# Six instead of four layer-norm finals behind up-projection products, and early splits at the start of down-projection

## The chip, the cores and the metric

The kernel runs on one core of one Trainium2 chip. The metric is the device time of one execution in microseconds (us), and a kernel's time is the median of its runs. Engines are called as in the profile: PE (TensorE), DVE (VectorE), ACT (ScalarE), POOL (GpSimd) and SP (SyncE, whose queue issues nearly all the transfers named here).

## The reference

One layer of a hybrid decoder, sequence 2048, model width 1024, feed-forward width 4096, all in float32. Cut to what matters here:

```python
proj = x @ w_in[l]
y_a, y_b, y_c, y_d = rwkv7(...), dilated_attention(...), ssd(...), hgrn2(...)
mix = jnp.concatenate([y_a, y_b, y_c, y_d], axis=-1) @ w_out[l]
x = _layer_norm(ALPHA * x + mix, ln1_w[l], ln1_b[l])
h = jnp.square(jax.nn.relu(x @ w_up[l]))
x = _layer_norm(ALPHA * x + h @ w_down[l], ln2_w[l], ln2_b[l])
```

The change touches the last four lines: the output projection `w_out`, the first layer norm, and the two feed-forward products.

## The kernel before, in words

**Numbers.** A float32 operand is split into a high part, which ACT copies to the type that PE multiplies (`split`, by `copy`), and a low part, raw minus high, which DVE makes, or POOL for every third one. A matrix product then is three PE instructions: high x high, high x low, low x high. A tile is 128 tokens; there are 16.

**Output projection and finals.** In the attention stage `out_part(t)` multiplies the six 128-row pieces of a tile that don't come from attention by their part of `w_out` and stores the sum `zF`. When the tile's attention is done, `out_final4(t)` merges the attention branches, loads `zF` into a buffer `z2`, adds the last two pieces' products (12 PE instructions `mm<-wh,yah` and the like), does the layer norm `lnorm` on DVE and ACT, stores the tile, transposes it by PE in two groups of four (`ident,z`), and stores the transposed tile in DRAM (`x1T`). It is cut into four pieces by `yield`. This is called a *final* below, numbered by its tile. `weave` hands such pieces out between the attention units, and what is left over runs behind the last unit. Finals 8 to 11 are in the last `weave`; finals 12 to 15 run in up-projection, each in four pieces, behind products 7t+6, 7t+8, 7t+13 and 7t+14 (t = 0 to 3).

**Up-projection** (`ffn_up`) takes the tokens in two halves (1024 each), and each half in 16 steps. A step makes a 2 x 2 block product out of seven products P1 to P7 instead of eight (sums and differences of blocks go into each). A product is 12 PE instructions of 512 columns into one PSUM bank. The four weight blocks `wr` of a step are loaded and made into seven split operands (`wh`, `wl`; `ws` are sums) by `ffn_w`; the bank results go through DVE, POOL and ACT (`q`, `u`, `c`) and are stored as seven combinations in DRAM (`H0P`, `H1P`). The first half's inputs come from tiles 0 to 7 (`ffn_x`), the second half's from tiles 8 to 15 (`ffn_x1`, in pieces during the first half's steps 7 to 14).

**Weight preparation.** Down-projection needs sums and differences of `w_down` blocks. `ffn_t` makes them for f = 0 to 15 in four `next` calls each and stores them in `TD`: 12 to 15 and 0 to 4 during `out_part`, on POOL alone; 5 in up-projection's steps 5 and 6, 6 to 11 in the second half, with DVE doing two of the four.

**Down-projection** (`ffn_down`) has 32 steps of seven products (PE instructions `bank<-x1h,hh` and the like). The seven weights are loaded and split up front (`x0h`, `x0l`, `x1h`, `x1l`), later exchanged by `change`. The inputs H are loaded into `xr` or `z2` and split four products ahead into buffers `hh` and `hl` of a pool `fd`, which lies over the pool of up-projection's weights. Loads, splits and products are written in one order, and a scheduler sets each engine's order from it. Each engine, and SP's queue, takes its instructions strictly in that order.

Of the kernel before, what the change touches and what calls it, by code (L numbers as in the profile page):

```python
# [84 lines left out]
class Body:  # L85
# [28 lines left out]
    def tt(self, eng, out, a, b, op):  # L114
        (self.nc.gpsimd if eng == "g" else self.nc.vector).tensor_tensor(out, a, b, op=op)  # L115

# [6 lines left out]
    def sub(self, eng, out, a, b):  # L123
        self.tt(eng, out, a, b, ALU.subtract)

# [7 lines left out]
    def copy(self, eng, out, in_):  # L133
        if eng == "a":
            self.nc.scalar.activation(out, in_, AF.Copy)  # L135
        elif eng == "g":
            self.nc.gpsimd.tensor_copy(out, in_)
        else:
            self.nc.vector.tensor_copy(out, in_)

# [17 lines left out]

    def load_split(self, src, n):

        h, out = n // 2, []
        for i in range(2):
            hi, lo = (self.t(self.wp, t, [P, self.wlen // 2], F32R, bufs=self.wbufs)[:, :h] for t in ("wh", "wl"))
            raw = self.t(self.rp, "raw", [P, self.wlen // 2], bufs=self.rbufs)[:, :h]
            self.nc.sync.dma_start(raw, src[:, h * i : h * i + h])
            self.split(raw, hi, lo)
            out.append((hi, lo))
        return h, out
# [7 lines left out]
    def split(self, raw, hi, lo):  # L176

        self.copy("a", hi, raw)
        self.rr += 1
        self.sub("g" if self.rr % 3 == 0 else "v", lo, raw, hi.bitcast(F32))  # L180

# [910 lines left out]
    def out_open(self, es, ef):  # L1092
# [5 lines left out]
        self.xT = [self.dp.tile([KT, P, 512], F32, name=f"x1T{i}") for i in range(seq // 512)]  # L1098
        load = lambda ks: [self.load_split(self.ap["w_out"][k], D) for k in ks]

# [5 lines left out]
        self.rbufs, self.wbufs, self.wlen = 4, 12, D  # L1106
        wo = load((0, 1, 4, 5, 6, 7))
        self.wp, self.wbufs = self.of, 4
        self.wo = wo + load((2, 3))
        self.nc.sync.dma_start(self.ln1, self.ap["lns"][0:2].partition_broadcast(P))  # L1110
# [284 lines left out]
    def ffn_down(self):  # L1395

        nc, tc, of = self.nc, self.tc, self.of
        nsteps = 32
        lns = self.t(of, "ln1", [P, 2, D], bufs=1)
        wtag = lambda n: "x1" if n in ("P1", "P6", "P4", "P3") else "x0"  # L1400
        chunk = lambda n, i: (i - self.OFF[n]) // 4 % 4
        with ExitStack() as es:
# [21 lines left out]
            def split_h(m):  # L1424
                if m < len(seq):
                    H[m] = [self.t(fd, x, [P, 512], F32R, bufs=6) for x in ("hh", "hl")]
                    self.split(raws.pop(m), *H[m])

# [21 lines left out]
            def prod(m):  # L1450
# [3 lines left out]
                for a, b, w, c in change:  # L1454
                    if a == m:
                        raws[w] = list(load_w(w, c))
                    if b == m:
                        split_w(w, raws.pop(w))
                ps = self.slot("py", [P, 512])
# [7 lines left out]

            places = ("xr", "xr", "wl", "wh", "wl", "wh", "wl")
            for q, (n, place) in enumerate(zip(("P1", "P6", "P2", "P7", "P5", "P4", "P3"), places)):
                rs = load_w(n, chunk(n, 0), place)  # L1470
                if place == "xr":
                    W[n] = [self.split_to(wtag(n), r) for r in rs]
                else:
                    split_w(n, list(rs))
                if q == 1:
                    for m in range(7):
                        load_h(m)
                if 0 < q < 5:
                    split_h(q - 1)
            for m in (7, 8, 9):  # L1480
                load_h(m)
            ys += [self.t(fd, f"y2_{n}", [P, 512]) for n in range(5, 14)]
            two = self.t(of, "x1t", [P, 2, 512], bufs=1)
            ys += [two[:, 0], two[:, 1]]
            for i in range(nsteps):
                hf, v, p = i // 16, i % 16 // 4, i % 4
                y = [[ys[4 * p + 2 * l + j] for j in range(2)] for l in range(2)]
# [28 lines left out]
                if i == 2:  # L1516
                    nc.sync.dma_start(lns, self.ap["lns"][2:4].partition_broadcast(P))
                if v == 3:
# [23 lines left out]
def body(ctx, tc, ap, seq=SEQ):  # L1542
# [74 lines left out]
    part = lambda t: (B.out_part(t), 7)  # L1617
    T = B.ffn_t((12, 13, 14, 15, *range(5)), False)

    def part_t(t):  # L1620
        for i, _ in enumerate(B.out_part(t)):
            if i in (0, 2, 4, 6) or i == 5 and t % 2:
                next(T)
# [8 lines left out]
    X = B.ffn_x()  # L1632
    B.weave([], units[40:], [final(8 + t) for t in range(4)])
    ea.close()
    with ExitStack() as e1:
        B.t(pool("pad", e1, side="right"), "pad", [P, 504])
        B.fw = pool("fw", e1, side="right", reuse_waits="tile")
        X1 = B.ffn_x1()
        T = B.ffn_t(range(5, 12), True)
        behind = {}  # L1640
        for t in range(4):
            it = B.out_final4(12 + t)
            for p in (6, 8, 13, 14):
                behind.setdefault(7 * t + p, []).append(it)
        B.ffn_up(0, X, lambda s: next(T) if s in (5, 6) else next(X1) if s in (7, 8, 9, 10, 11, 12, 13) else None,
                 lambda s: next(T) if s in (5, 6) else next(X1) if s in (8, 9, 11, 12, 14) else None, behind)
        B.ffn_up(1, next(X1), lambda s: next(T) if 1 < s < 14 else None, lambda s: next(T) if 1 < s < 14 else None)
# [82 lines left out]
```

## Time and profile before

| what | value |
| --- | --- |
| runs | 3148.49, 3129.91, 3138.72 us; median 3138.72 |
| profiled execution | 3125.35 us, span 3123.5 us |
| mean granted PE clock | 0.935 |
| PE busy | 2889.3 us, 93% of the span |
| DVE, POOL, ACT busy | 2154.9, 1607.3, 1357.1 us |
| attention stage ends, up-projection starts | about 1743 to 1760 us |
| down-projection starts | 2467 us |

The profiled execution is one run, 13.4 us faster than the median. In a timeline row stand the start, the duration, the engine, the line, the operation, output<-inputs, the shape and the count; in brackets the engine's idle time just before it and what ended that.

### The profile page before, as it was taken

To read this page: it belongs to the slowest core of one execution; us is meant where nothing else is said; L and a number is where in the kernel's file an instruction comes from. 1 tells how busy PE (TensorE), PEld (TensorE's weight loads), DVE (VectorE), ACT (ScalarE), POOL (GpSimd) and SP (SyncE) were. 2 spreads that over 40 slices of the span, in tenths; PEclk is the share of its full clock that TensorE was granted. 3 is DMA by queue.
4 is the path that set the end of the run, shared out by engine and by line. 5 is a ranking of instruction groups with operands and counts; after the bars stand their busy time and mean duration, and the time that the engine had idled before them with its cause. 6 is when DMAs were issued, how large, how long until landed. Compare 5 with 4: busy or idle time off the path is not lost. (4 is left out here: it accounts for less than half of the span.)

```text
span 3123.5 us, 46758 instructions
## 1 busy us (share of the span) xinstructions
PE 2889.3 (93%) x15524; PEld 2346.8 (75%) x15524; DVE 2154.9 (69%) x3794; ACT 1357.1 (43%) x2910; POOL 1607.3 (51%) x1466
## 2 busy tenths in 40 slices
PE   8899989889899999899999699999999899999996
PEld 6567777777677778777777477787788688878885
DVE  3457589778867765533445777678776677799777
ACT  3334334433443453334334444455455544554454
POOL 1333366455645645530223744646644577678666
PEclk9899888999899999699999799999999899999998
DMA  5434333333343354684455556658855866568653
GB/s 170 131 114 107 107 97 102 117 102 91 112 114 90 115 168 125 240 263 146 140 175 168 180 175 192 202 157 249 252 160 156 267 222 192 192 201 265 196 189 125
DMA packets 406083, 512.67 MB, mean 164 GB/s; under 512 B 34257, under 2 KB 234065, under 8 KB 405585
## 3 DMA queue, kind: packets, MB, share of 16 engines
q1 hardware_dynamic: 405840, 509.68, 52.8%
q8 instruction: 123, 2.02, 0.3%
q14 instruction: 120, 0.97, 0.1%
HBM read 353.64 MB, written 155.91 MB: 163 GB/s over the span
## 5 line engine op out<-in xcount | busy, mean ns | idle before, releaser
L112 PE MATMUL mm<-xh,wh 128*128 128x512 f32 x672 | 284.8, 426 | 30.7 <-ACT xh L135 16.9
L112 PE MATMUL mm<-xl,wh 128*128 128x512 f32 x672 | 284.6, 424 | 6.4 <-DVE xl L115 3.1
L112 PE MATMUL mm<-xh,wl 128*128 128x512 f32 x672 | 280.8, 418 | 2.7 <-DVE wl L115 2.6
L135 ACT ACTIVATE wh<-raw 128x512 fp32r<-128x512 f32 (+1 forms) x220 | 136.6, 629 | 177.3 <-PE mm L112 73.0
L112 PE MATMUL bank<-x1h,hh 128*128 128x512 f32 x512 | 200.8, 392 | 10.5 <-ACT hh L135 10.5
L115 POOL TENSOR_TENSOR y<-y,wh 128x512 f32<-128x512 f32 x112 | 173.8, 1562 | 58.0 <-ACT wh L135 31.1
L112 PE MATMUL bank<-x1h,hl 128*128 128x512 f32 x512 | 200.5, 392 | 2.1 <-DVE hl L115 2.1
L112 PE MATMUL bank<-x1l,hh 128*128 128x512 f32 x512 | 200.7, 392 | 0.8 <-DVE x1l L115 0.8
L112 PEld LDWEIGHTS mm<-xh,wh 128*128 128x128 f32 x672 | 134.4, 200 | 71.1 <-ACT xh L135 22.5
L112 PE MATMUL bank<-x0h,wh 128*128 128x512 f32 x384 | 155.8, 406 | 23.7 <-DVE c L115 18.3
L115 POOL TENSOR_TENSOR wl<-raw,wh 128x512 fp32r<-128x512 f32 (+1 forms) x74 | 101.5, 1373 | 135.9 <-ACT wh L135 131.4
L115 DVE TENSOR_TENSOR wl<-raw,wh 128x512 fp32r<-128x512 f32 (+1 forms) x146 | 117.5, 810 | 73.8 <-ACT wh L135 72.0
L112 PEld LDWEIGHTS mm<-xl,wh 128*128 128x128 f32 x672 | 134.9, 201 | 41.6 <-DVE xl L115 7.6
L112 PEld LDWEIGHTS mm<-xh,wl 128*128 128x128 f32 x672 | 134.3, 200 | 35.0 <-DVE wl L115 3.9
L112 PE MATMUL mm<-wh,xh 128*128 128x256 f32 (+1 forms) x512 | 155.1, 306 | 4.6 <-ACT stg L131 2.8
L112 PE MATMUL mm<-wl,xh 128*128 128x256 f32 (+1 forms) x512 | 154.6, 303 | 4.1 <-DVE wl L115 4.1
L112 PE MATMUL bank<-x0h,hh 128*128 128x512 f32 x384 | 151.8, 395 | 5.3 <-DVE x1t L128 4.9
L112 PE MATMUL bank<-x0h,hl 128*128 128x512 f32 x384 | 151.5, 394 | 5.5 <-DVE hl L115 5.5
L112 PE MATMUL bank<-x0l,wh 128*128 128x512 f32 x384 | 153.8, 400 | 0.0
L112 PE MATMUL bank<-x0h,wl 128*128 128x512 f32 x384 | 153.4, 400 | 0.0
L112 PE MATMUL mm<-wh,xl 128*128 128x256 f32 (+1 forms) x512 | 152.3, 299 | 0.0
L112 PE MATMUL bank<-x1l,wh 128*128 128x512 f32 x384 | 150.1, 391 | 2.3 <-DVE x1l L115 2.2
(474 smaller groups left out, 8773.8 us busy)
## 6 DMA issues: line engine op xcount, KB each, us to landing
raw<-in_w_ch SPq DMA_DIRECT2D x140, 256.0 KB, 3.0
wr<-in_w_up SPq DMA_DIRECT2D x128, 256.0 KB, 3.2
wl<-TDP SPq DMA_DIRECT2D x128, 256.0 KB, 3.6
wl<-in_w_down SPq DMA_DIRECT2D x104, 256.0 KB, 3.6
chF<-stg SPq DMA_DIRECT2D x68, 256.0 KB, 2.6
xraw<-in_xT SPq DMA_DIRECT2D x64, 256.0 KB, 3.6
z<-H0P SPq DMA_DIRECT2D x64, 256.0 KB, 3.7
z<-H1P SPq DMA_DIRECT2D x64, 256.0 KB, 3.8
```

The costliest lines, as they stand in the source:

```text
L112: return self.nc.tensor.matmul(out, lhsT, rhs, start=start, stop=stop)
L115: (self.nc.gpsimd if eng == "g" else self.nc.vector).tensor_tensor(out, a, b, op=op)
L135: self.nc.scalar.activation(out, in_, AF.Copy)
```

## The change

It has four parts.

1. Finals 10 and 11 leave the last `weave` and run behind products of up-projection, as 12 to 15 did: six finals, t = 0 to 5, at products 7t+6 to 7t+14. Final 15's last piece moves from product 35 to product 49.
2. Weight preparation f = 5 moves from up-projection's steps 5 and 6 into the `out_part` stage (five `next` per tile instead of four or five).
3. `w_out` is loaded by column halves: the left 512 columns of six row blocks, then their right ones, then the same for the last two blocks.
4. In down-projection the first three inputs (P1, P6, P2 of step 0) are split into the buffers `ln1` and `x1t`, which are free before `fd` is. The weights' splits are issued behind them (`issue_after`). The load of the second layer norm's parameters (`lns`, 1 MB, into `ln1`) moves from the top of the function to step 2, behind the last H load, and the two last accumulators in `x1t` are taken at step 1.

The helpers `copy`, `sub` and `tt` now return their instruction, which is left out of the diff.

```diff
@@ -156,10 +153,10 @@
         n = in_.shape[0]
         self.nc.tensor.transpose(out, in_, self.ident[:n, :n])
 
-    def load_split(self, src, n):
-
-        h, out = n // 2, []
-        for i in range(2):
+    def load_split(self, src, n, parts=2):
+
+        h, out = n // parts, []
+        for i in range(parts):
             hi, lo = (self.t(self.wp, t, [P, self.wlen // 2], F32R, bufs=self.wbufs)[:, :h] for t in ("wh", "wl"))
             raw = self.t(self.rp, "raw", [P, self.wlen // 2], bufs=self.rbufs)[:, :h]
             self.nc.sync.dma_start(raw, src[:, h * i : h * i + h])
@@ -175,9 +172,9 @@
 
     def split(self, raw, hi, lo):
 
-        self.copy("a", hi, raw)
+        a = self.copy("a", hi, raw)
         self.rr += 1
-        self.sub("g" if self.rr % 3 == 0 else "v", lo, raw, hi.bitcast(F32))
+        return a.ins, self.sub("g" if self.rr % 3 == 0 else "v", lo, raw, hi.bitcast(F32)).ins
 
     def rsqrt_small(self, x, n):
 
@@ -1096,7 +1093,6 @@
         self.zF = [self.dp.tile([P, D], F32, name=f"zF{t}") for t in range(seq // P)]
         self.TD = {n: [self.dp.tile([P, 512], F32, name=f"TD{n}_{f}") for f in range(16)] for n in ("P4", "P5", "P6", "P7")}
         self.xT = [self.dp.tile([KT, P, 512], F32, name=f"x1T{i}") for i in range(seq // 512)]
-        load = lambda ks: [self.load_split(self.ap["w_out"][k], D) for k in ks]
 
         self.of = ef.enter_context(tc.tile_pool(name="of", bufs=1))
         self.ln1 = self.t(self.of, "ln1", [P, 2, D], bufs=1)
@@ -1104,9 +1100,12 @@
         self.wp = es.enter_context(tc.tile_pool(name="wpo", bufs=2))
         self.op = es.enter_context(tc.tile_pool(name="op", bufs=1))
         self.rbufs, self.wbufs, self.wlen = 4, 12, D
-        wo = load((0, 1, 4, 5, 6, 7))
-        self.wp, self.wbufs = self.of, 4
-        self.wo = wo + load((2, 3))
+        h, wo = D // 2, {k: [] for k in range(8)}
+        for ks, self.wp, self.wbufs in (((0, 1, 4, 5, 6, 7), self.wp, 12), ((2, 3), self.of, 4)):
+            for j in range(2):
+                for k in ks:
+                    wo[k] += self.load_split(self.ap["w_out"][k][:, h * j : h * j + h], h, 1)[1]
+        self.wo = [(h, wo[k]) for k in (0, 1, 4, 5, 6, 7, 2, 3)]
         self.nc.sync.dma_start(self.ln1, self.ap["lns"][0:2].partition_broadcast(P))
 
     def out_mm(self, zt, yh, yl, ks, scale, stat=None):
@@ -1396,7 +1395,8 @@
 
         nc, tc, of = self.nc, self.tc, self.of
         nsteps = 32
-        lns = self.t(of, "ln1", [P, 2, D], bufs=1)
+        first = [self.t(of, "ln1", [P, 4, 512], F32R, bufs=1), self.t(of, "x1t", [P, 2, 512], F32R, bufs=1)]
+        first = [(first[i][:, j], first[i][:, j + 1]) for i, j in ((0, 0), (0, 2), (1, 0))]
         wtag = lambda n: "x1" if n in ("P1", "P6", "P4", "P3") else "x0"
         chunk = lambda n, i: (i - self.OFF[n]) // 4 % 4
         with ExitStack() as es:
@@ -1423,8 +1423,10 @@
 
             def split_h(m):
                 if m < len(seq):
-                    H[m] = [self.t(fd, x, [P, 512], F32R, bufs=6) for x in ("hh", "hl")]
-                    self.split(raws.pop(m), *H[m])
+
+                    H[m] = first[m] if m < 3 else [self.t(fd, x, [P, 512], F32R, bufs=6) for x in ("hh", "hl")]
+                    raws["split"] = self.split(raws.pop(m), *H[m])
+                    return raws["split"]
 
             def load_w(n, c, place=None):
                 for f in range(4 * c, 4 * c + 4):
@@ -1455,7 +1457,11 @@
                     if a == m:
                         raws[w] = list(load_w(w, c))
                     if b == m:
-                        split_w(w, raws.pop(w))
+                        with ExitStack() as e1:
+                            if m < 5:
+                                for ins in raws["split"]:
+                                    e1.enter_context(tc.issue_after(ins))
+                            split_w(w, raws.pop(w))
                 ps = self.slot("py", [P, 512])
                 hi, lo = H.pop(m)
                 for k in range(4):
@@ -1466,23 +1472,29 @@
                 return ps
 
             places = ("xr", "xr", "wl", "wh", "wl", "wh", "wl")
+            order = []
             for q, (n, place) in enumerate(zip(("P1", "P6", "P2", "P7", "P5", "P4", "P3"), places)):
                 rs = load_w(n, chunk(n, 0), place)
                 if place == "xr":
                     W[n] = [self.split_to(wtag(n), r) for r in rs]
                 else:
-                    split_w(n, list(rs))
+
+                    rs = list(rs)
+                    with tc.issue_after(order[0]), tc.issue_after(order[1]):
+                        split_w(n, rs)
                 if q == 1:
                     for m in range(7):
                         load_h(m)
                 if 0 < q < 5:
-                    split_h(q - 1)
+                    ins = split_h(q - 1)
+                    order = ins if q < 3 else order
             for m in (7, 8, 9):
                 load_h(m)
             ys += [self.t(fd, f"y2_{n}", [P, 512]) for n in range(5, 14)]
-            two = self.t(of, "x1t", [P, 2, 512], bufs=1)
-            ys += [two[:, 0], two[:, 1]]
             for i in range(nsteps):
+                if i == 1:
+                    two = self.t(of, "x1t", [P, 2, 512], bufs=1)
+                    ys += [two[:, 0], two[:, 1]]
                 hf, v, p = i // 16, i % 16 // 4, i % 4
                 y = [[ys[4 * p + 2 * l + j] for j in range(2)] for l in range(2)]
                 tl = [8 * hf + 4 * l + p for l in range(2)]
@@ -1514,7 +1526,9 @@
                 acc(1, 0, lambda: prod(m + 5), u3)
                 self.stt(y[0][1], y[0][1], 1.0, prod(m + 6), ALU.mult, ALU.add, stat[:, tl[0], 1:2] if v == 3 else None)
                 if i == 2:
-                    nc.sync.dma_start(lns, self.ap["lns"][2:4].partition_broadcast(P))
+                    lns = self.t(of, "ln1", [P, 2, D], bufs=1)
+                    with tc.issue_after(raws["last"]):
+                        nc.sync.dma_start(lns, self.ap["lns"][2:4].partition_broadcast(P))
                 if v == 3:
                     for l in range(2):
                         self.lnorm2(tl[l], y[l], stat[:, tl[l], :], lns)
@@ -1615,11 +1629,11 @@
     em.close()
     B.out_open(eo, ef)
     part = lambda t: (B.out_part(t), 7)
-    T = B.ffn_t((12, 13, 14, 15, *range(5)), False)
+    T = B.ffn_t((12, 13, 14, 15, *range(6)), False)
 
     def part_t(t):
         for i, _ in enumerate(B.out_part(t)):
-            if i in (0, 2, 4, 6) or i == 5 and t % 2:
+            if i in (0, 2, 4, 5, 6):
                 next(T)
             yield
 
@@ -1630,20 +1644,20 @@
     eo.close()
     B.ffn_open(ef)
     X = B.ffn_x()
-    B.weave([], units[40:], [final(8 + t) for t in range(4)])
+    B.weave([], units[40:], [final(8), final(9)])
     ea.close()
     with ExitStack() as e1:
         B.t(pool("pad", e1, side="right"), "pad", [P, 504])
         B.fw = pool("fw", e1, side="right", reuse_waits="tile")
         X1 = B.ffn_x1()
-        T = B.ffn_t(range(5, 12), True)
+        T = B.ffn_t(range(6, 12), True)
         behind = {}
-        for t in range(4):
-            it = B.out_final4(12 + t)
+        for t in range(6):
+            it = B.out_final4(10 + t)
             for p in (6, 8, 13, 14):
                 behind.setdefault(7 * t + p, []).append(it)
-        B.ffn_up(0, X, lambda s: next(T) if s in (5, 6) else next(X1) if s in (7, 8, 9, 10, 11, 12, 13) else None,
-                 lambda s: next(T) if s in (5, 6) else next(X1) if s in (8, 9, 11, 12, 14) else None, behind)
+        B.ffn_up(0, X, lambda s: next(X1) if s in (7, 8, 9, 10, 11, 12, 13) else None,
+                 lambda s: next(X1) if s in (8, 9, 11, 12, 14) else None, behind)
         B.ffn_up(1, next(X1), lambda s: next(T) if 1 < s < 14 else None, lambda s: next(T) if 1 < s < 14 else None)
     B.ffn_down()
     ef.close()
```

**PE, end of the attention stage and start of up-projection.** `av,aPT` is attention, `ident,z` and `ident,ya` are a final's transposes, `mm<-wh,yah` a final's product, and `bank<-x0h,wh` the first product instruction of up-projection. Before:

```order
L112 MATMUL bank_62<-av_16322,aPT_16338 128x64 x4
L157 MATMUL bank_66<-ident,aS_16347 128x128 x4
L112 MATMUL bank_62<-av_16322,aPT_16358 128x64 x4
L157 MATMUL bank_61<-ident,z_2797_16079 128x128 x8
L157 MATMUL bank_61<-ident,ya_16205 128x128 x2
L112 MATMUL mm_16243<-wh_12673,yah_16234 128x512
L112 MATMUL mm_16243<-wl_12674,yah_16234 128x512
```

After:

```order
L112 MATMUL mm_16280<-wh_12685,yal_16264 128x512
L112 MATMUL mm_16280<-wh_12691,yah_16263 128x512
L112 MATMUL mm_16280<-wl_12692,yah_16263 128x512
L112 MATMUL mm_16280<-wh_12691,yal_16264 128x512
L112 MATMUL bank_62<-x0h_15694,wh_16332 128x512
L112 MATMUL bank_62<-x0l_15695,wh_16332 128x512
L154 MATMUL bank_61<-ident,z_2831_16269 128x128 x4
L112 MATMUL bank_63<-x0h_15659,wh_16336 128x512
L112 MATMUL bank_63<-x0l_15660,wh_16336 128x512
```

Before, ahead of the first up-projection instruction stand final 9's transposes and then final 10's (transposes of `ya` and 12 products). After, it follows final 9's products, and final 9's transposes come behind it.

**PE, end of up-projection's step 0.** Before, ahead of its last two products (`bank_61`):

```order
L112 MATMUL bank_66<-x1l_15792,wh_16481 128x512
L112 MATMUL bank_66<-x1h_15791,wl_16482 128x512
L157 MATMUL bank_61<-ident,z_2828_16240 128x128 x4
L157 MATMUL bank_61<-ident,ya_16366 128x128 x2
L112 MATMUL mm_16404<-wh_12673,yah_16395 128x512
L112 MATMUL mm_16404<-wl_12674,yah_16395 128x512
```

and after, where step 0 ends:

```order
L112 MATMUL bank_61<-x1h_15753,wl_16355 128x512
L112 MATMUL bank_61<-x1h_15785,wh_16354 128x512
L112 MATMUL bank_61<-x1l_15786,wh_16354 128x512
L112 MATMUL bank_61<-x1h_15785,wl_16355 128x512
L154 MATMUL mm_16493<-ident,ya_16462 128x128 x2
L112 MATMUL bank_62<-x0h_15635,wh_16520 128x512
L112 MATMUL bank_62<-x0l_15636,wh_16520 128x512
```

Before, final 10's last transposes and all of final 11 stand inside step 0. After, step 0 is over when final 10 begins with its `ya` transposes, and step 1 follows at once.

**ACT, start of down-projection.** `x0h` and `x1h` are weight splits, `hh` input splits, `q<-bank` is the first product of up-projection's last step. Before:

```order
L135 ACTIVATE x1h_22288<-wl_22280 128x512
L135 ACTIVATE x1h_22292<-wl_22282 128x512
L135 ACTIVATE x1h_22296<-wl_22284 128x512
L135 ACTIVATE x1h_22300<-wl_22286 128x512
L135 ACTIVATE hh_22168<-xr_22156 128x512
L135 ACTIVATE hh_22196<-xr_22158 128x512
L135 ACTIVATE hh_22224<-xr_22160 128x512
L135 ACTIVATE hh_22252<-z_3849_22162 128x512
L135 ACTIVATE hh_22327<-z_3849_22162 128x512
```

After:

```order
L135 ACTIVATE wh_21978<-wr_21946 128x512
L131 ACTIVATE u_3792_21826<-u_3792_21826 128x512 x2
L135 ACTIVATE q_3815_21982<-bank_62 128x512
L135 ACTIVATE ln_3819_22099<-xr_22161 128x512
L135 ACTIVATE ln_3819_22099<-xr_22163 128x512
L135 ACTIVATE x0h_22183<-wl_22175 128x512
L135 ACTIVATE x0h_22187<-wl_22177 128x512
L135 ACTIVATE x0h_22191<-wl_22179 128x512
```

Before, the input splits are behind the last of the weight splits. After, those of P1 and P6 (into `ln`) are ahead of all of them; that of P2 (into `x1t`) is further ahead still. The later inputs' `hh` stay behind the weight splits.

More of the change, by code (lines that the diff above doesn't have):

```diff
@@ L114, in tt @@
     def tt(self, eng, out, a, b, op):
-        (self.nc.gpsimd if eng == "g" else self.nc.vector).tensor_tensor(out, a, b, op=op)
+        return (self.nc.gpsimd if eng == "g" else self.nc.vector).tensor_tensor(out, a, b, op=op)
     def mul(self, eng, out, a, b):
@@ L123, in sub @@
     def sub(self, eng, out, a, b):
-        self.tt(eng, out, a, b, ALU.subtract)
+        return self.tt(eng, out, a, b, ALU.subtract)
     def stt(self, out, a, s, b, op0, op1, acc=None):
@@ L134, in copy @@
         if eng == "a":
[L135 to L139, printed above, removed]
+            return self.nc.scalar.activation(out, in_, AF.Copy)
+        return (self.nc.gpsimd if eng == "g" else self.nc.vector).tensor_copy(out, in_)
     def c(self, name, a=None, b=None):
```

## The prediction, made before the changed kernel ran

> **What bounds the kernel now.** I read the page first, then the busy time by stretches of the span, then TensorE's (PE's) waits and its timeline in the stretches where it is not full, and last the other engines' timelines there.
>
> ```profile
> PE 2889.3 (93%) x15524; PEld 2346.8 (75%) x15524; DVE 2154.9 (69%) x3794; ACT 1357.1 (43%) x2910; POOL 1607.3 (51%) x1466
> ```
>
> ```profile
> core 0: us, PE busy (x) PEld busy (x) DVE busy (x) ACT busy (x) POOL busy (x), PEclk, DMA share, GB/s
> 1700.00:1750.00 50.00, 37.36 (x179) 29.39 (x179) 37.70 (x85) 26.75 (x71) 25.87 (x26) 0.74 0.54 176
> 1750.00:1800.00 50.00, 32.80 (x112) 23.52 (x111) 30.33 (x46) 13.89 (x28) 35.39 (x50) 0.74 0.54 177
> 2253.90:2440.40 186.50, 186.50 (x816) 152.99 (x815) 129.72 (x157) 91.81 (x160) 92.05 (x64) 1.00 0.52 153
> 2440.00:2460.00 20.00, 16.81 (x74) 13.51 (x72) 11.37 (x17) 11.68 (x21) 7.75 (x6) 1.00 1.03 359
> 2460.00:2500.00 40.00, 30.57 (x115) 24.45 (x116) 30.68 (x31) 20.30 (x35) 24.93 (x17) 0.79 0.89 295
> ```
>
> PE is the bound: full for the 186 us of plain up-projection. It has holes, and a granted clock of 0.74 to 0.79, in just the two transitions that the diff touches: attention to up-projection (1700 to 1800) and up- to down-projection (2456 to 2480). So a gain here is PE idle time removed, and moved PE work costs its full time.
>
> A product is 12 matrix instructions, a step of up-projection is 7 products, 84 instructions. ACT takes the first product of each step out of its bank; ten steps lie between these two:
>
> ```profile
> 2253.93 0.57 ACT L135 ACTIVATE q<-bank 128x512 f32<-128x512 f32 x1
> 2440.42 0.60 ACT L135 ACTIVATE q<-bank 128x512 f32<-128x512 f32 x1 [0.78 <-PE bank L112]
> ```
>
> So a step without stalls takes 186.5 / 10 = 18.65 us, an instruction 0.222 us.
>
> **The change, term 1: finals 10 and 11 leave the front of up-projection.** PE before, from final 9's transposes to the end of step 0 (start, length, in brackets the idle time before and what ended it):
>
> ```profile
> 1747.84 1.11 PE L157 MATMUL bank<-ident,z 128*128 128x128 f32 x4 [4.06 <-DVE z L128]
> ...
> 1759.78 0.50 PE L112 MATMUL bank<-x0h,wh 128*128 128x512 f32 x1 [1.06 <-ACT wh L135]
> ...
> 1774.17 0.66 PE L157 MATMUL bank<-ident,z 128*128 128x128 f32 x4 [1.70 <-DVE z L128]
> ...
> 1783.43 0.79 PE L112 MATMUL mm<-wh,yah 128*128 128x512 f32 x1 [0.47 <-ACT yah L135]
> ...
> 1794.54 1.11 PE L157 MATMUL bank<-ident,z 128*128 128x128 f32 x4 [5.63 <-DVE z L128]
> 1798.21 0.79 PE L112 MATMUL bank<-x0h,wh 128*128 128x512 f32 x1 [0.69 <-ACT x1t L135]
> ...
> 1807.12 0.38 PE L157 MATMUL mm<-ident,ya 128*128 128x128 f32 x2
> ```
>
> Each final is a dependent chain: products, DVE, layer norm, transposes. PE stands in it because nothing else is ahead in its order, and its idle time lowers the clock that is granted (0.74 in this window). In the changed order step 0's products follow final 9's products directly and final 10 starts behind the whole step.
>
> When can the first product start? Its weights take this path:
>
> ```profile
> 1746.27 0.32 SPq L509 DMA_DIRECT2D od<-ao  x1
> 1747.81 0.32 SPq L1166 DMA_DIRECT2D x<-z  x1
> 1748.18 1.25 SPq L1280 DMA_DIRECT2D wr<-in_w_up  x2
> ```
>
> ```profile
> 1758.39 0.68 DVE L115 TENSOR_TENSOR ws<-ws,wr 128x512 f32<-128x512 f32 x1
> ```
>
> The loads now stand behind the store `od<-ao` and no longer behind `x<-z`: 1748.18 - 1746.6 = 1.5 us sooner. On DVE the `ws` subtraction waited for the attention results of final 10, whose loads follow sooner as well; I take 1757.0 instead of 1759.78 (bounds 1753.5 an estimate with no wait but for the load, and 1759.8). Then: 84 x 0.222 = 18.65; final 9's 8 transposes, 0.66 to 1.11 us per four in the rows above and partly overlapped, 1.2 together; a half-rate start, 3.0, because PE idled before, as at the start of down-projection below, where half rate lasted the 6.1 us from 2472.36 to 2478.50; 1 us of late weights. Step 0 ends at 1757.0 + 18.65 + 1.2 + 3.0 + 1.0 = 1780.9, against 1807.12: **-26.3** (bounds -31, and -14 if the weights come 12 us late).
>
> The Trainium skill ("TensorE: Matmul & The Clock Gate", What's actually happening) gives about 3.4 us of sustained work until the full rate; by it the half-rate start would be 1.7 us rather than 3.0. The 6.1 us of the trace are longer, and I keep them.
>
> **Term 2: the same two finals are paid inside up-projection.** PE groups of 1810 to 1937, where four finals ran behind products:
>
> ```profile
> L112 PE MATMUL bank<-x1l,wh 128*128 128x512 f32 x91 | 35.4, 389 | 0.0
> L112 PE MATMUL bank<-x0l,wh 128*128 128x512 f32 x69 | 27.0, 392 | 0.0
> L112 PE MATMUL mm<-wh,yah 128*128 128x512 f32 x16 | 6.5, 405 | 1.8 <-DVE yal L115 1.8
> L157 PE MATMUL mm<-ident,z 128*128 128x128 f32 x32 | 4.9, 275 | 0.5 <-DVE z L128 0.5
> ```
>
> 3 x (91 + 69) = 480 up-projection instructions take 106.6 us at 0.222; the other 127 - 106.6 = 20.4 us are four finals, 5.1 each with their 2.3 us of waits. Two more: **+10.2** (bounds +8.4 without waits, +20 if each final costs twice). The cover for their DVE, ACT and POOL chains is step 0 to 6 of products; without it one holds PE for some 15 us, as final 11 above (1783.43 to 1798.21). The first input loads for the second half of up-projection need final 15. It now ends behind product 49 instead of 35, two steps later in order but at about the same time of day, and these inputs are wanted only at the end of the 16 steps.
>
> **Term 3: weight preparation f = 5 moves to the attention stage**, four POOL subtractions (at most 1.7 us each, by the POOL row in term 5) and 8 transfers. There POOL has room and PE does not wait for it:
>
> ```profile
> 1275.00:1410.00 135.00, 131.02 (x603) 105.60 (x602) 55.67 (x232) 54.06 (x208) 50.82 (x40) 0.81 0.76 252
> ```
>
> DMA at 0.76 is the only thing near full. **+1** (bounds -5, if it was this work in steps 5 and 6 that led to the 9.1 us of PE gaps quoted below, and +4). **Term 4, w_out by halves: 0.** The same bytes in another order; the last piece is issued long before the first use, and the products of this stage wait 0.2 us in all (SyncE's queue, then PE's group of 1300 to 1420):
>
> ```profile
> 1167.61 2.87 SPq L165 DMA_DIRECT2D raw<-in_w_out  x2
> ```
>
> ```profile
> L112 PE MATMUL mm<-wh,yh 128*128 128x512 f32 x69 | 29.4, 426 | 0.2 <-DVE yl L115 0.2
> ```
>
> **Term 5: first inputs of down-projection split into early free buffers.** PE, then ACT, POOL and SyncE's queue:
>
> ```profile
> 2456.42 0.39 PE L112 MATMUL bank<-x1h,wl 128*128 128x512 f32 x1
> 2467.35 0.80 PE L112 MATMUL bank<-x1h,hh 128*128 128x512 f32 x1 [10.54 <-ACT hh L135]
> ...
> 2472.36 0.80 PE L112 MATMUL bank<-x1h,hl 128*128 128x512 f32 x1 [2.08 <-DVE hl L115]
> ...
> 2478.50 0.39 PE L112 MATMUL bank<-x1h,hh 128*128 128x512 f32 x1
> ```
>
> ```profile
> 2465.49 1.28 ACT L135 ACTIVATE x1h<-wl 128x512 fp32r<-128x512 f32 x2 [0.74 <-DMA wl<-in_w_down]
> 2466.68 1.66 ACT L135 ACTIVATE hh<-xr 128x512 fp32r<-128x512 f32 x3
> 2468.24 1.65 ACT L135 ACTIVATE hh<-z 128x512 fp32r<-128x512 f32 x3
> ```
>
> ```profile
> 2470.06 1.70 POOL L115 TENSOR_TENSOR hl<-xr,hh 128x512 fp32r<-128x512 f32 x1
> ```
>
> ```profile
> 2450.16 0.33 SPq L1517 DMA_DIRECT2D ln<-in_lns  x1
> ```
>
> PE is idle for 10.5 us since the three `hh<-xr` are last on ACT, behind all weight splits. Now they come ahead of those, so P1, P6 and P2 (36 instructions, 8.0 us) run from 2456.8 to 2464.8. What is late next is P7: its `hh<-z` still stands behind the weight splits. ACT has three instructions fewer ahead of it (1.66 us), so about 2467, and its `hl` about 2469.5; 6 instructions fit between. At 2478.50 PE has then done 36 + 6 + (2478.5 - 2469.5) / 0.222 = 40, less 6 for a half-rate spell: 76; before it had done 6 + 15 = 21. (76 - 21) x 0.222 = 12.2. Bounds: 17 without any wait; 0 if the weights of the next steps are the bound (DMA share 1.03 and 0.89 in the two windows). I take **-10**, near the first, since the megabyte `ln<-in_lns` leaves this crowd of loads (now about 75 rows later on SyncE).
>
> Sum: -26.3 + 10.2 + 1 + 0 - 10 = **-25.1**. Against the profiled execution, 3125.35 us (span 3123.5), that is 3100.3. The runs' median, 3138.72, lies 13.4 above that execution, and the result is a median, so: 3138.7 - 25.1 = **3114**.
>
> **Rivals.** (B) *Down-projection's wait only moves*: weights, not inputs, end last, P7 waits until 2472 and term 5 is 0: -15.1, 3124. For it: ACT's 0.74 us for `in_w_down`. Against: 36 products are ready without it.
>
> (C) *Step 0 waits for its own weights*: finals 10 and 11 were the cover for the weight chain of steps 0 and 1, and term 1 falls by 10: -15, 3124. For it: `ws` came to DVE only at 1758.39. Against: the next gap behind 1759.78 is the one at 1774.17, and what ended it is a final's `z`, not a weight.
>
> (D) *Slower: the queues in order.* In each of steps 0 to 6 SyncE holds next weights behind a final's stores, and DVE holds bank evacuations behind its layer norm. Such a jam is in the trace at 1936 to 1986, where the second half's inputs are made:
>
> ```profile
> PE bank L112 <- DVE c L115: 8.7, 2, 5.5
> PE bank L112 <- DVE u L115: 3.6, 1, 3.6
> ```
>
> It cost 3.6 + 5.5 = 9.1 us in one step. If all six finals' steps have one, +55: 3138.7 - 25 + 55 = 3169; it decides from 25 / 6 = 4.2 us per final on. Against: four finals at 1810 to 1937 had 2.3 us of waits together.
>
> (E) *DVE and POOL hold each other up* so that two more finals cost more than PE's time. DVE's layer-norm rows:
>
> ```profile
> 1746.50 1.28 DVE L128 SCALAR_TENSOR_TENSOR z<-z,stat,ln 128x1024 f32<-128x1024 f32 x1
> ...
> 1766.70 2.30 DVE L128 SCALAR_TENSOR_TENSOR z<-z,stat,ln 128x1024 f32<-128x1024 f32 x1
> ```
>
> 1.0 us longer while POOL subtracts. Seven such DVE instructions per final at 1.0 each, all reaching PE: 14 for two, -11, 3128. Against it, again, those 2.3 us. The Trainium skill ("SBUF — State Buffer", Who interferes with whom) has an exclusive port for DVE instructions with both inputs in SBUF against POOL's; the two rows agree.
>
> **How the numbers follow.** The forecast has 0.55 (its own range 3102 to 3124), B 0.14, C 0.13, D 0.09, E 0.09. Under 0.5% (15.7 us) a measurement of this kernel can't tell a difference from none. Faster takes 0.53 of the forecast, half of B and C (0.13) and 0.02 of E: 0.68; slower is D; same the rest, 0.23. Range: the forecast's low side with better bounds of terms 1 and 5 (-31 + 10 - 12 = -33, and 9 us of run-to-run spread): 3096; up to E and that spread: 3137.
>
> **What would show it.** Right: no `mm<-wh,yah` between final 9 and the end of step 0; step 0 over near 1781; the wait for `hh` at 2456 down from 10.5 to some 2 us; steps with a final at 23 to 25 us. Wrong: PE gaps `<-ACT wh` or `<-DVE wl` in steps 0 and 1 (C), a wait for `x0h`, `x1h` behind P2 (B), `<-DVE c` or `u` gaps over 4 us in steps 0 to 6 (D).

## The result: 0.56% faster, 17 of the 25 us

The changed kernel takes 3119.49 us (median of 20 runs, 3098.27 to 3130.13) against 3136.87 us before (20 runs, 3117.76 to 3148.49): ratio 0.9944, 95% interval 0.9925 to 0.9962. It is 17.4 us faster by the medians. I had forecast 25 us and 3114 us, with 3096 to 3137 as the range.

The two profiled executions seem to deny it: the span was 3123.5 us before and is 3125.0 us now. Their pages differ little; this is the one after, and the one before stands in the prediction:

```profile
PE 2908.3 (93%) x15524; PEld 2364.4 (76%) x15524; DVE 2161.0 (69%) x3792; ACT 1354.0 (43%) x2910; POOL 1614.6 (52%) x1468
```

The reason stands in SyncE's queue at the first load of `w_out`, before and after. Up to that row no engine's order was changed:

```profile
1135.79 0.33 SPq L165 DMA_DIRECT2D raw<-in_w_out  x1
```

```profile
1153.00 0.33 SPq L162 DMA_DIRECT2D raw<-in_w_out  x1
```

The same work took 17 us longer in the second execution. Over the fourteen profiles told of in this document that row lies between 1135.8 and 1162.0 us. So I compare stretches that begin there. The marks are that load, and ACT's rows that take a step's first product out of its bank: the second (step 1 of up-projection), the 17th (its second half), the 23rd and the 32nd (the last step), then the row with the 29th and 30th load `z<-H0P` in steady down-projection. Before (the 32nd stands in the prediction) and after:

```profile
1810.63 0.58 ACT L135 ACTIVATE q<-bank 128x512 f32<-128x512 f32 x1
2140.15 0.58 ACT L135 ACTIVATE q<-bank 128x512 f32<-128x512 f32 x1
2273.36 0.58 ACT L135 ACTIVATE q<-bank 128x512 f32<-128x512 f32 x1
```

```profile
2589.20 0.90 SPq L1421 DMA_DIRECT2D z<-H0P  x2
```

```profile
1801.84 0.58 ACT L135 ACTIVATE q<-bank 128x512 f32<-128x512 f32 x1
2143.99 0.58 ACT L135 ACTIVATE q<-bank 128x512 f32<-128x512 f32 x1
2283.93 0.58 ACT L135 ACTIVATE q<-bank 128x512 f32<-128x512 f32 x1
2449.60 0.60 ACT L135 ACTIVATE q<-bank 128x512 f32<-128x512 f32 x1 [0.79 <-PE bank L112]
```

```profile
2590.80 0.90 SPq L1421 DMA_DIRECT2D z<-H0P  x2
```

Both kernels were profiled a second time (the runs `r_before` and `r_after` below). In us:

| stretch | before, twice | after, twice | difference of the means |
| --- | --- | --- | --- |
| start: first `w_out` load to step 1 | 674.8, 675.9 | 648.8, 644.6 | -28.7 |
| first half: step 1 to the second half | 329.5, 329.4 | 342.1, 342.4 | +12.8 |
| second half, first six steps | 133.2, 135.4 | 139.9, 143.7 | +7.5 |
| second half, the rest | 167.1, 166.0 | 165.7, 165.8 | -0.8 |
| start of down-projection | 148.8, 147.5 | 141.2, 140.3 | -7.4 |
| rest | 534.3, 534.4 | 534.2, 533.9 | -0.3 |
| sum | 1987.7, 1988.6 | 1972.0, 1970.8 | -16.8 |

The sum agrees with the medians. The first transition gave what was forecast, the second somewhat less, and one row was in no forecast: the second half's first six steps became 7.5 us longer.

PE at the first transition, after:

```profile
1767.60 0.39 PE L112 MATMUL mm<-wh,yal 128*128 128x512 f32 x1
1775.63 0.80 PE L112 MATMUL bank<-x0h,wh 128*128 128x512 f32 x1 [7.64 <-ACT wh L135]
...
1777.18 1.12 PE L154 MATMUL bank<-ident,z 128*128 128x128 f32 x4 [0.33 <-DVE z L128]
...
1798.37 0.38 PE L154 MATMUL mm<-ident,ya 128*128 128x128 f32 x2
```

The last product instruction of final 9 is followed by 7.64 us of waiting for weights, and then step 0 runs through in 22.7 us. The waits for the finals' `z` and `x1t` that cut step 0 up before are gone: behind 1777.18 PE waits for neither until the step ends.

PE's waits at the start of down-projection (2449 to 2529), after:

```profile
PE bank L112 <- POOL hl L115: 2.1, 1, 2.1
PE bank L112 <- ACT hh L135: 1.9, 1, 1.9
PE bank L112 <- DVE x1l L115: 1.1, 1, 1.1
PE bank L112 <- ACT x1h L135: 0.9, 1, 0.9
```

The first two are waits of P7, which follows the 36 instructions of P1, P6 and P2:

```profile
2476.28 0.50 PE L112 MATMUL bank<-x0h,hh 128*128 128x512 f32 x1 [1.89 <-ACT hh L135]
2480.89 0.80 PE L112 MATMUL bank<-x0h,hl 128*128 128x512 f32 x1 [2.14 <-POOL hl L115]
```

The 10.5 us for `hh` and 2.1 for `hl` have become 6.0 us in four pieces, two of them (`x1h`, `x1l`) for the next step's weights.

### The profile page after: what moved, and what is told of

Same layout as the page of the kernel before. It is cut to its first block, busy times and chain, and to the rows that moved or that the text cites. A ratio compares the mean times of both kernels' runs of the same rounds, so it can differ in the third digit from the quotient of the medians.

```text
span 3125.0 us, 46714 instructions
## 1 busy us (share of the span) xinstructions
PE 2908.3 (93%) x15524; PEld 2364.4 (76%) x15524; DVE 2161.0 (69%) x3792; ACT 1354.0 (43%) x2910; POOL 1614.6 (52%) x1468
## 5 line engine op out<-in xcount | busy, mean ns | idle before, releaser
L112 PE MATMUL mm<-xh,wh 128*128 128x512 f32 x672 | 284.0, 425 | 31.6 <-ACT xh L135 17.4
L112 PE MATMUL bank<-x0l,hh 128*128 128x512 f32 x380 | 151.4, 398 | 0.0
```

The costliest lines, as they stand in the source:

```text
L112: return self.nc.tensor.matmul(out, lhsT, rhs, start=start, stop=stop)
```

## The experiments

All ratios are against the kernel before, timed on the same chip. For most of these kernels the interval is as wide as the effect sought, so the verdicts rest on the stretches of one profile each, which the pairs above show to repeat within some 4 us (the start, the second half's first six steps) or some 1 us (the others).

**The same two kernels again (r_before, r_after).**

> The kernel before once more, for the spread of the stretches. Theory 1 (the first six steps of up-projection's second half, 133.2 us in before and 139.9 in the changed kernel, differ by when transfers land, not by the change): within 133 to 141 us, and not the same as the first time. Rival (the change makes them 6 us longer): 133 to 135 again. The start (first w_out load to step 1), 674.8 us, within 3 us again.

> The changed kernel once more. Theory 1: the same six steps within 133 to 141 us. Rival: 139 to 142 again. The start, 648.8 us, and down-projection's start, 141.2 us, within 3 us again.

Measured: before 135.4 us in the six steps, after 143.7. The starts were 675.9 and 644.6 us, down-projection's start 140.3 us. The rival holds: the 6 us and more belong to the change, and one profile is good to some 4 us there.

**Finals 10 and 11 alone (e1).**

```diff
-    B.weave([], units[40:], [final(8 + t) for t in range(4)])
+    B.weave([], units[40:], [final(8), final(9)])
-        for t in range(4):
-            it = B.out_final4(12 + t)
+        for t in range(6):
+            it = B.out_final4(10 + t)
```

> The kernel before, with finals 10 and 11 behind up-projection products and nothing else changed (weight preparation f = 5 stays in steps 5 and 6). Theory 1 (the gain at the first transition is final 10's and 11's chains): first w_out load to the first product of step 1 is 26 us shorter than before (674.8 us there), step 1 to the second half's first product 10 to 13 us longer (329.5 us), the rest as before: in all 13 to 16 us, ratio 0.995 to 0.996. Rival (f = 5 had to move, since it shares buffer x1t with the finals): the stretch of up-projection's first half is over 17 us longer and nothing or little is left, ratio over 0.997.

Measured: 3127.76 us, ratio 0.9997 (0.9973 to 1.0021); the plain ratio of the medians, against 3137.35 on that chip, is 0.9969, so the timed runs leave open how much of the gain is left. The start is 647.4 us, 28 less than before, as theory 1 has it. But the first half is 350.3 us, 20.8 more than before and 8.0 more than in the changed kernel: there the rival's number came. From the load on it takes 1982.3 us, and only 6 of the 28 are left. PE's waits in the first half of this kernel (1797 to 2148), and of the changed one (1802 to 2144):

```profile
PE bank L112 <- DVE c L115: 13.8, 3, 7.1
PE mm L157 <- DVE z L128: 10.0, 5, 3.4
```

```profile
PE bank L112 <- DVE c L115: 9.5, 3, 4.1
PE mm L154 <- DVE z L128: 6.1, 4, 2.8
```

The 8.2 us between these pairs are the 8.0 of the stretch. The loss stands where f = 5 does: by ACT's rows, steps 6 and 7 take 26.1 and 27.0 us here, against 21.3 and 23.1 in the changed kernel. Weight preparation f = 5 in steps 5 and 6 and the finals that now reach these steps are in each other's way: the move of f = 5 is part of the gain and not a side matter. That the shared buffer `x1t` is the reason, and not DVE's and the transfers' load, I did not separate.

**Weight preparation and `w_out` alone (e3).**

```diff
+        for ks, self.wp, self.wbufs in (((0, 1, 4, 5, 6, 7), self.wp, 12), ((2, 3), self.of, 4)):
+            for j in range(2):
+                for k in ks:
+                    wo[k] += self.load_split(self.ap["w_out"][k][:, h * j : h * j + h], h, 1)[1]
...
-    T = B.ffn_t((12, 13, 14, 15, *range(5)), False)
+    T = B.ffn_t((12, 13, 14, 15, *range(6)), False)
-            if i in (0, 2, 4, 6) or i == 5 and t % 2:
+            if i in (0, 2, 4, 5, 6):
```

> The kernel before, with w_out loaded left halves first and weight preparation f = 5 in the out_part stage; finals and down-projection as before. Theory 1: both are worth nothing, every stretch within 3 us of before, ratio 0.999 to 1.001. Rival (the 5 us that the changed kernel lost in up-projection's second half, 305.6 against 300.3 us, come with f = 5): the second half is 5 us longer here too, and the first half up to 9 us shorter, since the waits of step 6 go.

Measured: 3137.23 us, ratio 0.9993 (0.9963 to 1.0024), a time from which nothing can be told. The start is 669.5 us, 6 less than before, the first half 325.8, 4 less, the second half's six steps 134.3. So theory 1 misses by a little, and f = 5 is worth 4 us in the first half even without the finals. It does not bring the second half's loss: there the rival fails. The 6 us at the start may be f = 5's too, since three of its loads stood ahead of step 0 before (1754.01 to 1758.47), or `w_out`'s; the two weren't tried apart.

**Down-projection's start alone (e2).** All of the diff's `ffn_down`, nothing else:

```diff
+        first = [self.t(of, "ln1", [P, 4, 512], F32R, bufs=1), self.t(of, "x1t", [P, 2, 512], F32R, bufs=1)]
...
+                    H[m] = first[m] if m < 3 else [self.t(fd, x, [P, 512], F32R, bufs=6) for x in ("hh", "hl")]
```

> The kernel before, with the early splits of down-projection's first inputs and the later load of lns only. Theory 1: from the last up-projection step's first product to the steady down-projection 8 us less than before (280.4 us there), everything ahead unchanged: ratio 0.9975. Rival (the gain at the second transition exists only because finals moved the phase ahead of it): under 3 us, ratio 0.999 to 1.001.

Measured: 3134.85 us, ratio 0.9995 (0.9969 to 1.0022). Down-projection's start is 140.3 us, 8 less than before: theory 1 there. But the second half's first six steps are 139.3 us, 5 more than the mean of the two before. Most of the loss comes with this part, in a stretch that ends 166 us ahead of the last step, where the work starts that it was written for.

**lns loaded early (e4).**

```diff
-                if i == 2:
+                if i == 0:
                     lns = self.t(of, "ln1", [P, 2, D], bufs=1)
```

> The changed kernel with the 1 MB load of lns at step 0 of down-projection instead of step 2, so that it is among the weight loads again. Theory 1 (transfers end last once the inputs are split early): the start of down-projection is 2 to 4 us longer than in the changed kernel (272.6 us to the steady state), ratio about 0.9955 to before. Rival (ACT's order alone sets it): no difference, ratio 0.9944 as the changed kernel.

Measured: 3123.62 us, ratio 0.9965 (0.9938 to 0.9992); down-projection's start 140.9 us, as in the changed kernel. The load in this kernel, and in the changed one:

```profile
2491.82 0.37 SPq L1531 DMA_DIRECT2D ln<-in_lns  x1
```

```profile
2529.20 0.38 SPq L1531 DMA_DIRECT2D ln<-in_lns  x1
```

Behind ACT's row of the last step's first product that is 44.9 us here (row at 2446.97) and 79.6 in the changed kernel. In the kernel before it was 9.7 (2450.16), although the load is written at step 2 there too: only its buffer was claimed at the top. The waits for `hh` and `hl` end 31.3 us behind that mark in the changed kernel (2480.89) and sooner than the load here too, so this edit did not put the megabyte back among the loads that these wait with. It shows that 35 us earlier or later behind them makes no difference. What the megabyte's leaving of the first crowd is worth, the reason that I gave for trusting term 5, no run shows.

**P1 first in step 0 (e7).**

```diff
-    B.weave([], units[40:], [final(8), final(9)])
+    B.weave([], units[40:], [final(8), (B.out_final(9), 1)])
```

Final 9 then uses the products' two buffers, bank 0 is free, and PE's order begins with P1.

> The changed kernel with final 9's transposes in the two buffers of the products (mm) instead of bank 0, so that P1 of step 0, whose weights need neither POOL nor DVE before ACT, comes first in PE's order and its 12 instructions run while P6's weights are made. Theory 1 (what is left of the gap ahead of step 0, 7.6 us, is the wait for P6's weights): 2 to 4 us less from the first w_out load to step 1 (648.8 us in the changed kernel), ratio to before 0.9935. Rival (all weights of step 0 come equally late, PE then waits inside the step): no difference.

Measured: 3116.32 us, ratio 0.9936 (0.9909 to 0.9963), not to be told from the changed kernel by time. PE at the start of step 0:

```profile
1764.51 0.50 PE L112 MATMUL bank<-x0h,wh 128*128 128x512 f32 x1 [1.50 <-ACT wh L135]
...
1770.58 0.50 PE L112 MATMUL bank<-x0h,wh 128*128 128x512 f32 x1 [1.20 <-ACT wh L135]
```

The 7.64 us are 2.7 now, so most of what was left of that gap was the wait for one product's weights. How much time the 5 us less of waiting gave is not shown: the start is 643.9 us, 2.8 less than the changed kernel's mean, but that kernel's two lie 4.2 apart, and the three other kernels with this edit (e10, e11 and e12 below) have 648.6, 650.1 and 639.2.

**Seven finals (e8).** Final 9 too, and the second half's inputs one step later:

```diff
-    B.weave([], units[40:], [final(8), final(9)])
+    B.weave([], units[40:], [final(8)])
...
-        for t in range(6):
-            it = B.out_final4(10 + t)
+        for t in range(7):
+            it = B.out_final4(9 + t)
```

> The changed kernel with final 9 behind products too (seven finals), and the second half's inputs made one step later. Theory 1 (the gain was the chains of finals 10 and 11 standing ahead of P1, and final 9's products now run while PE would wait for weights anyway): the start is 0 to 2 us shorter than in the changed kernel, up-projection's first half 5 to 7 us longer, ratio to before 0.9955 to 0.996, slower than the changed kernel. Rival (each final taken out of the front is worth some 13 us, as the two were worth 27): start 8 to 13 us shorter, ratio 0.992.

Measured: 3125.00 us, ratio 0.9963 (0.9941 to 0.9986). The start is 648.4 us, no shorter than the changed kernel's 644.6 and 648.8; the first half 354.8, 12.5 longer. The rival is out. Theory 1 holds in kind, with a cost twice what I gave, the later inputs among it. At the start PE now waits for the final ahead:

```profile
1762.63 1.12 PE L154 MATMUL bank<-ident,z 128*128 128x128 f32 x4 [11.28 <-DVE z L128]
```

Final 8's transposes still stand in front, with nothing to cover them. A final taken out is worth its chain only where something else is ready to run.

**What is longer in the second half: the queue of loads? (e9)** In the changed kernel SyncE's queue holds one more load there, `xr<-H0P` for down-projection's input 7, between the stores and weights of a step.

```diff
+            with tc.issue_after(raws["w"]):
                 for m in (7, 8, 9):
                     load_h(m)
```

(`raws["w"]` is the last load of P2's weights.)

> The changed kernel with the loads of inputs 7 to 9 of down-projection issued behind the weights of P2, so that the load of input 7 into xr no longer stands in SyncE's queue in the middle of up-projection's second half, where it waits for the early split of P2's input to free its buffer. Theory 1 (that waiting load holds the stores and weight loads behind it): the first six steps of the second half come down from 140 to 144 us to 134 to 137 us, all other stretches as in the changed kernel, ratio to before 0.993. Rival (those 6 us come from the phase in which the half starts): 140 to 144 us again, ratio 0.9944.

Measured: 3114.99 us, ratio 0.9943 (0.9917 to 0.9969); the six steps 139.6 us. The load is gone from there and the time is not: theory 1 fell. ACT's row of this kernel, and of the changed one, at that place:

```profile
2250.56 0.63 ACT L135 ACTIVATE x1t<-xr 128x512 fp32r<-128x512 f32 x1 [4.71 <-DMA xr<-H0P]
```

```profile
2257.86 0.63 ACT L135 ACTIVATE x1t<-xr 128x512 fp32r<-128x512 f32 x1 [3.74 <-DMA xr<-H0P]
2258.39 0.61 ACT L131 ACTIVATE c<-c 128x512 f32<-128x512 f32 x1
```

What is left there is the early split of P2's input itself. Its buffer is free early, so it was put early in ACT's order, and there ACT waits for its load (3.7 to 5.2 us in the nine profiles with the early split), with the step's evacuation `c<-c` behind it. In the kernel before (`r_before`) the same `c<-c` waits only for its own operand:

```profile
2261.06 0.63 ACT L131 ACTIVATE c<-c 128x512 f32<-128x512 f32 x1 [2.25 <-DVE c L115]
```

**P1 first and the late loads together (e10).**

> Both: P1 first in step 0 of up-projection, and the late loads of inputs 7 to 9. Theory 1 (two separate waits on the path that sets the end): the start 2 to 4 us and the second half 4 to 6 us shorter than in the changed kernel, ratio to before 0.992. Rival (one wait takes the other's place): no better than one of them alone, 0.9935.

Measured: 3108.66 us, ratio 0.9923 (0.9897 to 0.995), the lowest here, but its stretches (start 648.6, six steps 141.4, from the first `w_out` load to the end 1972.3 us) are those of the changed kernel. So neither theory's gain is seen in them. Since the late loads do nothing, I take this as the kernel with P1 first, within the spread.

**P7's split ahead of weight splits, on top of e10 (e11).**

```diff
-                    order = ins if q < 3 else order
+                    order = ins if q < 3 or q == 4 else order
```

> As the one before, and the split of P7's input ahead of the weight splits of P4 and P3 on ACT. Theory 1 (ACT's order is what is left of the wait at the start of down-projection, 1.9 us for hh and 2.1 us for hl): the start of down-projection comes down from 141 us by 2 to 4 us, ratio to before 0.991. Rival (the weights of P4 and P3 then end last): 141 us again or longer.

Measured: 3119.36 us, ratio 0.9956 (0.993 to 0.9983); down-projection's start 145.0 us, 4 longer. PE's waits there:

```profile
PE bank L112 <- POOL hl L115: 4.9, 1, 4.9
PE bank L112 <- DVE hl L115: 3.0, 1, 3.0
```

The wait for `hh` is gone and 7.9 us for `hl` have come. The rival is right that it is no better, though not by its mechanism: the low halves end last, not the weights.

**P2's split behind those of P1 and P6, on top of e7 (e12).**

```diff
+                    with ExitStack() as e2:
+                        if q == 3:
+                            for x in order:
+                                e2.enter_context(tc.issue_after(x))
+                        ins = split_h(q - 1)
```

> The kernel with P1 first in step 0 of up-projection, and the split of P2's first input behind those of P1 and P6 on ACT, so that it no longer stands in ACT's and DVE's order in the middle of up-projection's second half, where it waits 3.7 to 4.8 us for its load. Theory 1 (that split, in order on ACT, holds the evacuations of a step): the first six steps of the second half come down from 140 to 144 us to 134 to 137 us, the start of down-projection stays at 140 to 143 us, ratio to before 0.992. Rival (the loads of this stretch are late anyway): 139 us or more again, ratio 0.9935.

Measured: 3113.51 us, ratio 0.994 (0.9913 to 0.9967). The six steps are 136.9 us, inside what theory 1 gave, where the nine profiles with the early split have 139.0 to 143.7 and the four without it 133.2 to 136.8. The split now stands 190 us later, at the end of the second half, and waits for nothing:

```profile
2447.99 1.15 ACT L135 ACTIVATE ln<-xr 128x512 fp32r<-128x512 f32 x2 [1.97 <-PE bank L112]
2449.05 0.62 ACT L135 ACTIVATE x1t<-xr 128x512 fp32r<-128x512 f32 x1
```

The split stood in the fifth of the six steps. From ACT's 21st row to its 23rd, that is over the fifth and sixth step, the nine profiles with the early split take 42.7 to 47.0 us and the five without it, this one included, 39.8 to 41.8. In the four steps ahead they take 95.5 to 97.3 and 93.3 to 95.5; there every engine's order is the same in all of them, so this smaller difference is not the split's. The rows here, then the 21st before and in the changed kernel, whose 23rd stand above:

```profile
2235.91 0.58 ACT L135 ACTIVATE q<-bank 128x512 f32<-128x512 f32 x1
2277.71 0.58 ACT L135 ACTIVATE q<-bank 128x512 f32<-128x512 f32 x1
```

```profile
2233.46 0.58 ACT L135 ACTIVATE q<-bank 128x512 f32<-128x512 f32 x1
```

```profile
2239.61 0.58 ACT L135 ACTIVATE q<-bank 128x512 f32<-128x512 f32 x1
```

Down-projection's start is 141.6 us, as before the edit. From the first `w_out` load to the end this kernel takes 1961.7 us, the least of all, against 1972.0 and 1970.8 for the changed kernel; some 5 of these 10 us are a shorter attention stage (592.5 us to the ninth `x1T<-x1t`, against 598.8 and 595.8), which the edit does not touch. Its timed runs do not part it from the changed kernel.

## Why the prediction was right, and where it was short

**Term 1 (-26.3): right, step by step.** From the first `w_out` load I had put the first product at 1757.0 - 1135.8 = 621.2 us and the end of step 0 at 645.1; they came at 1775.63 - 1153.00 = 622.6 and 645.4. The start became 28.7 us shorter, and finals alone (e1) gave 28. Some of the 28.7 may be term 3's, since e3 has 6 us there. (In the working, 1748.18 - 1746.6 is 1.6 and not 1.5; the sum does not use it.)

**Term 2 (+10.2): right in kind, too small.** The first half's +12.8 is near it only because term 3 came out the other way in the same stretch, which is luck. With f = 5 out of both, the two more finals cost 342.2 - 325.8 = 16.4 us (changed kernel and e3), and with f = 5 in both 20.8 (e1). Six finals' steps carry 6.1 us of PE waits for `z`, where four carried 0.5. These are the finals' own chains, no longer covered as well as in the four that I took the price from; why not, I don't know.

**Term 3 (+1): wrong in sign.** I costed f = 5 by where it goes and gave its removal only as a bound (-5). Its removal is the point: 8.0 us of the first half beside six finals (e1 against the changed kernel), 4 beside four (e3), and there 10 with the start, where `w_out` may have a part. Term 4 is not told apart from it.

**Term 5 (-10): -7.4.** The mechanism is shown by e2, -8 by itself. I had allowed some 3 us of waits for P7; there were 4.0, and 2.0 more for the next step's weights. Less the 9.18 us between the two kernels' marks of the last step, P7's first `hh` product came at 2467.1, as forecast (about 2467), and its first `hl` product at 2471.7 and not about 2469.5: the low half, on POOL, was the late one. Whether the later megabyte helped, the support that I named, no run shows (e4).

**The step that failed most is one that is not in the sum.** I followed the inputs' splits to where they are wanted and wrote that P2's "is further ahead still", without asking what it waits for there. It holds ACT, in order, in the second half. Rival D had the mechanism, an engine's queue held by one instruction that waits, at another place (layer norms in steps 0 to 6) and with another price. How much of the 7.5 us it is: 5.6 lie in the fifth and sixth step (45.6 us in the mean of the changed kernel's two profiles, 40.0 before). Some 2 to 4 of these are the split's: e7 (43.9) and e12 (41.8) differ in it alone, and against the changed kernel's mean the two kernels with the finals and without the early split, e1 and e12, take 4.0 less (41.6). The rest came with the finals. The 1.9 that are left lie in the four steps ahead, where no engine's order was changed. I have no cause for these two parts; the phase of the transfers, which changes with the start, is a guess.

Rival B is out: what came at 2471.7 was P7's low half and not its weights, and term 5 is far from 0. Rival C's mark is there, the 7.64 us `<-ACT wh` ahead of step 0's first product, but the 621.2 us already held this wait, and inside the step PE waits for no weights. E is not seen as a separate cost: behind products, one of a final's two 1024-column layer-norm rows on DVE takes 1.3 to 1.4 us and the other 2.2 to 2.3 in both kernels, so its longer rows were in the price of term 2.

## What to carry to other kernels

An instruction whose buffer comes free early isn't an early instruction: before it is moved ahead on an engine that runs in order, look up when its input lands, and what stands behind it. When work is taken out from in front of a bound engine, ask what it covered and what is ready to take its place; two finals were worth 28 us at the start because step 0's 84 instructions could run in their place, and a third was worth nothing. Where identical work differs by tens of us from run to run, measure stretches between marks that both kernels have, not spans.

## What was not expected of the hardware

The work ahead of the first changed instruction took 1135.8 to 1162.0 us over fourteen profiles, a spread of 2.3%, while the last stretch, 534 us of steady down-projection, repeats within 1.1 us (533.5 to 534.6). The mean granted clock of the shortest of these executions was 0.935, of the longest 0.926. Whether the clock is the cause or follows from waits I have not tried.
